# Down projection of a gated feed-forward: eleven Strassen pairs in groups of six and five in place of two plain blocks and ten pairs

## The chip, the cores and the metric

One core of one Trainium2 chip runs the whole program. The metric is device microseconds (us) of one execution on that core. Engines are named as the profile names them: PE (TensorE matmuls), PEld (its weight loads), DVE (VectorE), ACT (ScalarE), POOL (GpSimd), SP (SyncE, which here issues most of the loads).

## What is computed

A trunk of two layers over 1024 tokens of width 1024: differential attention in layer 0, latent attention in layer 1, each followed by a gated feed-forward with a causal convolution of width 3; one RMSNorm at the end. What the change touches is the last product of the feed-forward:

```python
def conv_ffn(h, w_up, conv_w, conv_b, w_down):
    u = h @ w_up
    c = lax.conv_general_dilated(
        u, conv_w[:, None, :].astype(u.dtype), window_strides=(1,),
        padding=[(CONV_WIDTH - 1, 0)], dimension_numbers=('NWC', 'WIO', 'NWC'),
        feature_group_count=u.shape[-1]) + conv_b
    g, val = jnp.split(c, 2, axis=-1)
    return (jax.nn.silu(g) * val) @ w_down      # (1024 x 2816) @ (2816 x 1024)

for i in range(DEPTH):                           # DEPTH = 2
    ...
    x = x + conv_ffn(h, ffn_w_up[i], ffn_conv_w[i], ffn_conv_b[i], ffn_w_down[i])
```

## The kernel before

**Numbers.** Everything is fp32. A factor is split into a high part (`hi`, L128, a cast on ACT) and a low part (`lo`, L131, a subtraction on DVE), and a product is three matmuls of 128x512, `mm3`, at L120, L121 and L122. So each new factor of 128x512 costs one cast on ACT and one subtraction on DVE.

**Down projection** (`down`). The hidden width 2816 is 22 blocks of 128 rows. Gated blocks arrive from the up projection through HBM: the convolution's `store` (L1097) writes block f to `g_d[f]` from ACT's queue, and `fetch` (L1265) loads halves of it, and of the weight rows, on SP's queue. Two neighbouring blocks form a pair, four quarters A11 to A22 of 128x512 of the gated values and four, B11 to B22, of the weights. A pair's product is made by seven products M1 to M7 of 128x512 factors (Strassen-Winograd) in place of eight; their factors (`DOWN`) are quarters or sums of quarters (`SUMS`; S1 to S4 of A, T1 to T4 of B), made on DVE (L1275). One M of one pair is 12 matmuls: four token tiles by three. The pairs are worked in groups: for each M, in the order `FOLLOW` (M2, M1, M5, M6, M3, M7, M4), all pairs of the group are added up in PSUM banks, and then `evict` (L1441) adds the four banks to the resident residual tiles X on DVE. M3, M6, M7 and M4 go on in the banks of an earlier M (`ONTO`), so they wait until those have been read. `todo` lists the products in this order, numbered i from 0.

**The two plain blocks.** 22 blocks are eleven pairs, but before the change only ten pairs are worked so, in groups of five and five (`GROUPS`). Blocks 0 and 1 are plain: their 96 matmuls per layer (two blocks, eight token tiles, two halves, three each) stand first, right behind the last product of the up projection. Four of their sixteen tiles lie in the first M2's banks, and the other twelve are taken by adds into X (`taken`, L1387).

**Up projection's closing.** At the point where the down projection's matmuls begin, the last hidden block f=21 is not ready yet. `pieces` (handed over as `before`) are its remaining steps: `closing` (L1203, an add on DVE that reads the temporary `U2`), the convolution's base and taps (L1084, L1088), `silu` (L1091), `gated` (L1094) and `store` (L1097). `down` calls one piece after each of its first products.

**What sets the order.** SP's order is written out: from the first fetch to the middle of the plain products its queue runs in the order of the program (`manual_schedule` over SP). ACT's order is likewise the program's in the up projection and its closing (`region`). `advance(i + DEPTH - 1)` prepares the factors of products ahead: cast, subtraction and then the sums that `MAKE` (keyed by the product's number in its group) puts there, at most two steps at a call. Tile names: u, s and h tiles are places in SBUF, S, b and u (as a matmul's output) are PSUM. In SP's rows `s<-x_d` is a load of 1 MB of the residual X (L1321), `<-g_d` and `<-in_ffn_down` are quarters of 256 KB. A DMA's landing is counted on one of eight counters, named DMAHW0 to DMAHW7 in the order of instructions, taken in turn; a new DMA on a counter waits for the last one's landing there.

Of the kernel before, what the change touches and what calls it, by code (L numbers as in the profile page):

```python
# [56 lines left out]
class Trunk:  # L57
# [946 lines left out]
    def up(self, layer, pl, g_d, follow):  # L1004
# [214 lines left out]
    GROUPS = (range(1, 6), range(6, 11))  # L1219
# [10 lines left out]
    MAKE = {4 + j: [(j, "S1"), (j, "T1")] for j in range(5)}  # L1230
    MAKE |= {o: [(x // 4, ("S3", "T3", "S2", "T2")[x % 4]) for x in xs] for o, xs in zip(range(9, 18), (range(0, 3), range(3, 6), *(range(i, i + 2) for i in range(6, 20, 2))))}
    for j in range(5):
        MAKE.setdefault(18 + j, []).append((j, "S4"))
        MAKE.setdefault(23 + j, []).append((j, "T4"))

    LAST = (0, 2, 1, 3)

    LIE = {"A12": (0, 0), "B21": (0, 1), "A11": (1, 0), "B22": (1, 1), "A22": (2, 0), "B11": (2, 1), "A21": (3, 0), "B12": (3, 1)}
    LIE2 = {"A12": "A11", "B21": "B11", "A11": "A12", "B11": "B22", "A21": "A21", "B12": "B12", "A22": "A22", "B22": "B21"}

    NEXT = {"M3": ["A12", "A11", "B11"], "M7": ["B21", "A21", "B12"], "M4": ["A22", "B22"]}

    def down(self, layer, pl, g_d, x_d, done, ahead):
# [3 lines left out]
        ring, temps = self.ring(*pl.down), self.ring(*[f"h{i}" for i in (9, 8, 3, 0, 5, 6, 7, 4, 1, 2)])  # L1247
# [10 lines left out]
        def fetch(j, name):  # L1258
            unit, half = self.LIE[name if j < 6 else self.LIE2[name]]
            k = (j - 1) % 5, unit  # L1260
            if k not in places:
                place = pl.units[unit][k[0]]
                places[k] = self.at(place, [P, D]) if isinstance(place, str) else place()
            blocks[j, name] = places[k][:, half * 512 : half * 512 + 512]
            nc.sync.dma_start(blocks[j, name], source(j, name))  # L1265

        def value(j, name):

            if name not in self.SUMS:
                return blocks[j, name]  # L1270
            if (j, name) not in made:
                x, y, op, place = self.SUMS[name]
                x, y = value(j, x), value(j, y)
                made[j, name] = temps([P, 512]) if place is None else blocks[j, place]
                nc.vector.tensor_tensor(made[j, name], x, y, op)  # L1275
            return made[j, name]

        def sums(i):
            n, o = divmod(i, len(todo) // 2)
            if n < 2:  # L1280
                for x, name in self.MAKE.get(o, ()):
                    value(self.GROUPS[n][x], name)

# [7 lines left out]
        def low(i):  # L1291
# [6 lines left out]
            if n == 0:  # L1298
                for name in self.NEXT.get(m, []):
                    fetch(j + 5, name)  # L1300
# [14 lines left out]
        X, raws, plain = [], [], []  # L1315
# [7 lines left out]
        def fetch_plain(src, *pieces):  # L1323

            w = D // len(pieces)
            for x, piece in enumerate(pieces):
                nc.sync.dma_start(piece, src[:, x * w : x * w + w])
            raws.append(pieces)

        def high_plain(i):  # L1330
            plain.append(ring([P, 2, D], F32R))
            w = D // len(raws[i])
            for x, piece in enumerate(raws[i]):
                self.hi(plain[i][:, 0, x * w : x * w + w], piece)

        def low_plain(i):
            w = D // len(raws[i])
            for x, piece in enumerate(raws[i]):
                c = slice(x * w, x * w + w)
                self.lo(plain[i][:, 1, c], piece, plain[i][:, 0, c])  # L1340


        w_down = a["ffn_down"][layer]
        order = self.tc.manual_schedule(engines={mybir.EngineType.SP})
        order.__enter__()
        unit = lambda i: self.at(pl.raw[i], [P, D])
# [5 lines left out]
        fetch_plain(g_d[1], self.at(pl.w[4], [P, D]))  # L1352
        fetch_plain(w_down[P : 2 * P, :], self.at("h12", [P, 512]), self.at("h13", [P, 512]))
        high_plain(1)
        yield
        def fetch_all(j, *names):
            for name in names:
                fetch(j, name)

        fetch_all(1, "A12", "B21")  # L1360
        yield
        fetch_all(2, "A12", "B21")
        fetch_all(3, "A12", "B21")
        high_plain(2)
        yield
        low_plain(0)
        low_plain(1)
        fetch_x(1)
        high_plain(3)
        yield  # L1370
        low_plain(2)
        fetch_all(4, "A12", "B21")
        fetch_x(1)
        yield
        low_plain(3)
        fetch_x(1)
        fetch_all(5, "A12", "B21")
        fetch_x(1)
        for j in range(1, 6):
            fetch_all(j, "A11", "B11")  # L1380
        fetch_all(1, "A21", "B12", "A22")
# [7 lines left out]
        two = [self.big() for _ in range(2)]  # L1389
        ahead_of = [s[:, cols] for s in two for cols in (first, rest)]  # L1390

        def plain_product(out, t, b, j, last):
            g, w = plain[j : j + 2]
            tok, cols = slice(t * P, t * P + P), slice(b * 512, b * 512 + 512)
            self.mm3(out, g[:, 0, tok], g[:, 1, tok], w[:, 0, cols], w[:, 1, cols], j == 0, last)

        older = []
        pairs = [[(0, 1), (1, 1)], [(2, 1), (3, 1)]] + [[(t, 0), (t, 1)] for t in range(4, NT)]
        for x, pair in enumerate(pairs):
            now = [(at_, self.bank("u" if x % 2 and b else "b")) for b, at_ in enumerate(pair)]  # L1400
            both = [(2 * x + q, ahead_of[2 * x + q]) for q in range(2)] if x < 2 else []
            for j in (0, 2) if x == 0 else (None,):
                for q, out in both:
                    for i in (0, 2) if j is None else (j,):
                        plain_product(out, q, 0, i, False)
                for (t, b), out in now:
                    for i in (0, 2) if j is None else (j,):
                        plain_product(out, t, b, i, i == 2)
            taken(older)
            older = now  # L1410
            if before:
                for f in before.pop(0):
                    f()
            if x:
                if x > 1:
                    low(x - 2)
                high(x - 1)
# [915 lines left out]
```

## Time and profile before

| what | before |
| --- | --- |
| median of 3 runs (lowest, highest) | 2365.13 us (2365.07, 2366.61) |
| the profiled execution: its own time, its span | 2365.86 us, 2364.0 us |
| PE busy | 2342.8 us (99% of the span), 12146 matmuls |
| DVE busy | 1898.2 us (80%) |
| ACT, POOL busy | 1252.7 us (53%), 577.6 us (24%) |
| first plain matmul of the down projection, layer 0 | 980.95 us |

Times are read from the profiled execution, on its own clock, which starts with the span. Where the text names a time such as +2.7, it counts from 980.95 us, the start of the down projection's matmuls in layer 0 (called its start below).

### The profile page before, as it was taken

Reading aid. Unit: us, or ns where it says so; the run is one execution under the profiler, and the core shown is the slowest. Engines: PE = TensorE matmul, PEld = TensorE weight load, DVE = VectorE, ACT = ScalarE, POOL = GpSimd, SP = SyncE. Lnnn points to the kernel's source line nnn. Section 1 sums busy time; section 2 is a strip of 40 time slices with the busy share of each in tenths; the row PEclk is TensorE's granted clock in tenths of the full one; section 3 lists DMA queues with packets and bytes.
Section 4 is the critical chain, followed back from the end, with each engine's and each line's share of the span. In section 5 each row is a group of like instructions: output and inputs, shape, how many; then the busy total and the mean of one; then the engine's idle time right before and its main releaser. Section 6 shows DMA issues by size and latency. Waiting matters only on the chain.

```text
span 2364.0 us, 32924 instructions
## 1 busy us (share of the span) xinstructions
PE 2342.8 (99%) x12146; PEld 1977.4 (84%) x12146; DVE 1898.2 (80%) x3148; ACT 1252.7 (53%) x2308; POOL 577.6 (24%) x464
## 2 busy tenths in 40 slices
PE   9999999999999999999999999999999999999998
PEld 7888888788888888888899889988888888888887
DVE  6777878859888888899844888886588888888997
ACT  5666666745444444444444777775454444444444
POOL 4545444323000000000132666664420000000001
PEclk9999999999999999999999999999999999999999
DMA  4111111342222222643222211124322222228502
GB/s 148 41 37 37 49 37 54 112 134 87 93 84 81 80 81 89 231 149 118 93 82 63 72 31 41 41 88 120 105 79 90 88 81 80 81 86 288 170 10 81
DMA packets 95665, 213.42 MB, mean 90 GB/s; under 512 B 8712, under 2 KB 33936, under 8 KB 95504
## 3 DMA queue, kind: packets, MB, share of 16 engines
q1 hardware_dynamic: 86304, 183.51, 23.6%
q10 hardware_dynamic: 9200, 27.80, 3.2%
q8 instruction: 96, 1.57, 0.3%
q14 instruction: 65, 0.53, 0.1%
HBM read 158.85 MB, written 52.43 MB: 89 GB/s over the span
## 4 chain that ended last, share of the span: by engine, by line
PE 94%; DVE 3%; DMA 1%; ACT 1%; issue 1%; POOL 0%; POOLq 0%; ACTq 0%; DVEq 0%; SPq 0%
PE S L122 14%; PE S L120 14%; PE S L121 13%; PE b L120 9%; PE b L121 9%; PE b L122 9%; PE u L120 5%; PE u L122 5%; PE u L121 5%; PE S L1878 3%; PE b L264 2%; PE u L2034 1%; PE b L1924 1%; PE u L2033 1%; DVE s L131 1%
## 5 line engine op out<-in xcount | busy, mean ns | idle before, releaser
L168 POOL TENSOR_TENSOR st<-st,mhalf 128x1 f32<-128x1 f32 x56 | 33.0, 590 | 1288.6 <-DVE st L165 1273.5
L120 PE MATMUL S<-s,u 128*128 128x512 f32 (+1 forms) x800 | 302.1, 378 | 0.2 <-ACT u L1110 0.2
L122 PE MATMUL S<-s,u 128*128 128x512 f32 (+1 forms) x800 | 301.5, 377 | 0.1
L121 PE MATMUL S<-s,u 128*128 128x512 f32 (+1 forms) x800 | 301.4, 377 | 0.0
L128 ACT CAST u<-h 128x512 fp32r<-128x512 f32 (+1 forms) x194 | 115.8, 619 | 266.7 <-DVE h L1031 262.8
L120 PE MATMUL b<-s,u 128*128 128x512 f32 x588 | 231.0, 393 | 1.1 <-DVE u L131 0.4
L122 PE MATMUL b<-s,u 128*128 128x512 f32 x588 | 229.3, 390 | 0.0
L121 PE MATMUL b<-s,u 128*128 128x512 f32 x588 | 229.3, 390 | 0.0
L1088 DVE SCALAR_TENSOR_TENSOR u<-u,conv,u 128x1023 f32<-128x1023 f32 (+1 forms) x176 | 225.0, 1279 | 0.8 <-ACT u L1084 0.7
L128 ACT CAST s<-u 128x512 fp32r<-128x512 f32 (+3 forms) x253 | 157.0, 658 | 123.1 <-issue 25.2
L150 POOL TENSOR_TENSOR u<-u,st 128x512 f32<-128x512 f32 (+7 forms) x160 | 173.3, 1092 | 160.8 <-DVE st L2019 107.9
L128 ACT CAST u<-b 128x512 fp32r<-128x512 f32 (+1 forms) x256 | 134.8, 547 | 92.3 <-PE b L1924 57.7
L131 DVE TENSOR_TENSOR u<-b,u 128x512 fp32r<-128x512 f32 (+1 forms) x256 | 158.6, 631 | 23.8 <-ACT u L128 22.6
L120 PEld LDWEIGHTS S<-s,u 128*128 128x128 f32 x800 | 150.6, 188 | 27.9 <-ACT u L1110 0.5
L122 PEld LDWEIGHTS S<-s,u 128*128 128x128 f32 x800 | 150.6, 188 | 27.7 <-DVE u L131 0.3
L121 PEld LDWEIGHTS S<-s,u 128*128 128x128 f32 x800 | 150.7, 188 | 27.3
L131 DVE TENSOR_TENSOR s<-u,s 128x512 fp32r<-128x512 f32 (+2 forms) x229 | 157.9, 729 | 14.6 <-ACT s L128 14.5
L120 PE MATMUL u<-s,s 128*128 128x512 f32 (+1 forms) x404 | 163.7, 405 | 1.1 <-DVE s L131 0.9
L122 PE MATMUL u<-s,s 128*128 128x512 f32 (+1 forms) x404 | 156.9, 388 | 0.0
L121 PE MATMUL u<-s,s 128*128 128x512 f32 (+1 forms) x404 | 156.3, 387 | 0.0
L1091 ACT ACTIVATE u<-u 128x1024 f32<-128x1024 f32 x44 | 46.7, 1062 | 200.3 <-DVE u L1088 200.3
L131 DVE TENSOR_TENSOR u<-h,u 128x512 fp32r<-128x512 f32 x171 | 118.1, 691 | 32.4 <-ACT u L128 31.5
(291 smaller groups left out, 6336.5 us busy)
## 6 DMA issues: line engine op xcount, KB each, us to landing
u<-in_ffn_up SPq DMA_DIRECT2D x88, 512.0 KB, 4.1
g_d<-u ACTq DMA_DIRECT2D x44, 512.0 KB, 2.6
u<-g_d SPq DMA_DIRECT2D x64, 256.0 KB, 4.9
u<-in_ffn_down SPq DMA_DIRECT2D x64, 256.0 KB, 5.2
s<-in_da_wqkv SPq DMA_DIRECT2D x23, 512.0 KB, 3.3
x_d<-u SPq DMA_DIRECT2D x16, 512.0 KB, 2.6
s<-x_d SPq DMA_DIRECT2D x8, 1024.0 KB, 10.8
u<-in_x SPq DMA_DIRECT2D x8, 512.0 KB, 6.2
```

Source lines behind the costliest of these rows:

```text
L120: mm(out, lh, rl, start=first, stop=False, skip_group_check=onto)
L121: mm(out, lh, rh, start=False, stop=False, skip_group_check=onto)
L122: mm(out, ll, rh, start=False, stop=last, skip_group_check=onto)
L128: self.nc.scalar.copy(out, src)
L131: (eng or self.nc.vector).tensor_sub(out, src, hi.bitcast(F32))
L150: self.nc.gpsimd.tensor_mul(x, x, s.to_broadcast(list(x.shape)))
L168: nc.gpsimd.tensor_tensor(r, s, self.mhalf, ALU.pow)
L264: self.nc.tensor.transpose(ps[:, j * P : (j + 1) * P], probs[t][:, k : k + P], self.ident)
L1088: nc.vector.scalar_tensor_tensor(t[half][:, back:], u[half][:, : S - back], w, t[half][:, back:], ALU.mult, ALU.add)
L1091: nc.scalar.activation(t[0], t[0], AF.Silu)
L1878: nc.tensor.matmul(sc[c][:, b : b + m], q[rows, qp, qs], kt[rows, kp, :m], start=x == 0, stop=x == 2)
L1924: k.nc.tensor.transpose(ps[:, j * P : (j + 1) * P], self.e[t][0][:, c : c + P], k.ident)
```

## The change

The plain blocks go; blocks 0 and 1 become pair 0, and the eleven pairs are worked in groups of six and five. The first M2 takes the plain products' place behind the up projection: with the first product none is issued, with the second pairs 0 and 1 are issued together (`now`). Per layer that is 84 matmuls for blocks 0 and 1 in place of 96. The adds of `taken` go (12 per layer), as do the five subtractions of the plain factors; seven products of pair 0 bring 14 subtractions and eight sums. All sums are made in place, in a quarter that is no longer wanted, so that the h tiles that held S1 and T1 are free for quarters of pairs 0, 1 and 5. `MAKE` becomes `plan`: in a group of six, S3, S1 and T1 of pair j are made at product 10 + j, S2 and T2 at 16 + j, S4 and T3 at 22 + j, T4 at 28 + j. `advance` makes one step at a call for the first six products and two after. The ring of prepared factors keeps eight places, the places of the quarters (`pl.units`) are new. Cut to its core (the lines of `evict` and of the sums are L1383 and L1282 in the changed kernel, fetches L1272 and L1329; lines up to L1211 are as before):

```diff
-    GROUPS = (range(1, 6), range(6, 11))
+    GROUPS = (range(6), range(6, 11))
...
-        "S1": ("A21", "A22", ALU.add, None), "T1": ("B12", "B11", ALU.subtract, None),
-        "S3": ("A11", "A21", ALU.subtract, "A21"), "S2": ("A22", "S3", ALU.subtract, "A11"), "S4": ("A12", "S2", ALU.subtract, "A12"),
-        "T3": ("B22", "B12", ALU.subtract, "B12"), "T2": ("T3", "B11", ALU.add, "B11"), "T4": ("B21", "T2", ALU.subtract, "B21"),
+        "S3": ("A11", "A21", ALU.subtract, "A11"), "S1": ("A21", "A22", ALU.add, "A21"), "T1": ("B12", "B11", ALU.subtract, "B11"),
+        "S2": ("A22", "S3", ALU.subtract, "A21"), "T2": ("B22", "T1", ALU.subtract, "B11"), "S4": ("A12", "S2", ALU.subtract, "A12"),
+        "T3": ("B22", "B12", ALU.subtract, "B12"), "T4": ("B21", "T2", ALU.subtract, "B21"),
...
+    def plan(self, size):
+
+        plan = {}
+        for j in range(size):
+            for o, names in ((2 * size - 2, ("S3", "S1", "T1")), (3 * size - 2, ("S2", "T2")), (4 * size - 2, ("S4", "T3")), (5 * size - 2, ("T4",))):
+                plan.setdefault(o + j, []).extend((j, name) for name in names)
+        return plan
...
-        ring, temps = self.ring(*pl.down), self.ring(*[f"h{i}" for i in (9, 8, 3, 0, 5, 6, 7, 4, 1, 2)])
+        ring = self.ring(*pl.down)
...
-                made[j, name] = temps([P, 512]) if place is None else blocks[j, place]
+                made[j, name] = blocks[j, place]
...
-        fetch_plain(g_d[0], unit(0))
-        fetch_plain(w_down[:P, :], unit(1))
+        fetch_all(range(4), "A12", "B21")
         yield
-        high_plain(0)
+        high(0)
         yield
...
+        fetch_all([4], "A12", "B21")
+        high(1)
         yield
...
+        fetch_all([5], "A12", "B21")
         yield
...
+        fetch_all([0, 1], "A11", "B11")
+        high(2)
         yield
...
+        low(0)
+        low(1)
+        fetch_all([2], "A11", "B11")
         fetch_x(1)
-        high_plain(3)
+        high(3)
         yield
...
+        low(2)
+        fetch_all([3, 4], "A11", "B11")
         fetch_x(1)
         yield
...
+        low(3)
+        high(4)
+        fetch_all([5], "A11", "B11")
+        fetch_all(range(4), "A21", "B12", "A22", "B22")
+        fetch_x(2)
         before, region = yield
-
-        def taken(pairs):
-            for (t, b), y in pairs:
-                x = X[t // 2][:, t % 2, b * 512 : b * 512 + 512]
-                nc.vector.tensor_add(x, x, y)
...
                 for j in group:
+                    now = [j]
+                    if i < 2:
+                        now = group[:2] if i else []
                     for q in range(4):
-                        products(banks[m][q], n, m, j, q, group)
+                        for x in now:
+                            products(banks[m][q], n, m, x, q, group)
+                    if before:
+                        for f in before.pop(0):
+                            f()
+                        if not before:
+                            fetch_all([4, 5], "A21", "B12", "A22", "B22")
+                            order.__exit__(None, None, None)
...
-                    advance(i + DEPTH - 1)
+                    advance(i + DEPTH - 1, 1 if i < len(self.GROUPS[0]) else 2)
...
-            down=slots(0, 1, 4, 5, 13, 12, 10, 11), X=slots(2, 3, 6, 7),
+            down=slots(0, 1, 10, 11, 12, 4, 5, 13), X=slots(2, 3, 6, 7),
...
+        pl.units = [[("h12", "h13"), ("h3", "h0"), "u14", "u15", "u9", "u0"], [("h1", "h2"), *units(1, 12, 4, 5, 13)],
+                    ["u11", s8[1], s9[1], "u3", "u7", "u6"], ["u10", s8[0], s9[0], "u8", "u2", ("h4", "h5")]]
```

How the instructions stand shows at three places, all in layer 0 around the up projection's closing. A row's last part names the semaphores that it waits for.

SP, in the change, from the last fetches for M2 on (h_1597 and h_1598 are pair 0's A11 and B11, in the temporaries h1 and h2; h2 has held the `U2` that `closing` reads; L1329 is a load of X; u_1604 and u_1605 are A11 and B11 of pairs 3 and 4, s_1612 the A21, A22, B12 and B22 of pair 1):

```order
L1272 DMA h_1597_9156<-g_d_142 128x512 [waits DMAHW5_49,DVE_49]
L200 DMA h_1742_10868<-in_mla_g 128x384 [waits DMAHW6_49,DVE_49]
L1272 DMA h_1598_9157<-in_ffn_down 128x512 [waits DMAHW0_49,DVE_49]
L1272 DMA u_1599_9160<-g_d_142 128x512 [waits DMAHW1_49,PE_49]
L1272 DMA u_1599_9160<-in_ffn_down 128x512 [waits DMAHW2_49]
...
L1329 DMA s_1602_9188<-x_d_139 128x2x1024 [waits DMAHW5_49,PE_49]
...
L1329 DMA s_1606_9215<-x_d_139 128x2x1024 [waits DMAHW2_49]
...
L1272 DMA s_1612_9247<-in_ffn_down 128x512 [waits DMAHW2_49]
L1272 DMA s_1612_9247<-g_d_142 128x512 [waits DMAHW3_49]
L1272 DMA s_1612_9247<-in_ffn_down 128x512 [waits DMAHW4_49]
```

Behind the fetch into h_1598 stand, in the change, 17 fetches of 256 KB and two loads of X up to and with the row of s_1612 that takes the counter DMAHW3. The same queue before, at the place where the plain blocks' fetches end:

```order
L1265 DMA u_1596_9150<-in_ffn_down 128x512 [waits DMAHW2_49]
L1321 DMA s_1598_9172<-x_d_139 128x2x1024 [waits DMAHW3_49,PE_49]
L1265 DMA u_1600_9192<-g_d_142 128x512 [waits DMAHW4_49]
L1265 DMA u_1600_9192<-in_ffn_down 128x512 [waits DMAHW5_49]
L1321 DMA s_1601_9195<-x_d_139 128x2x1024 [waits DMAHW6_49]
L1321 DMA s_1603_9215<-x_d_139 128x2x1024 [waits DMAHW7_49,PE_49]
```

Before, none of these rows waits for DVE; in the change the third row of the piece waits for it, and the loads of X stand behind that row.

ACT, in the change, around the store of the last hidden block (s_1625 is product 9, s_1631 product 10, s_1636 product 11):

```order
L128 CAST s_1625_9357<-u_1604_9209 128x512 [waits DMAHW6_49,PE_49]
L128 CAST s_1625_9357<-u_1604_9209 128x512 [waits DMAHW7_49]
L1097 DMA g_d_142<-u_1580_9067 128x1024 [waits DMAHW3_49,DVE_49]
L128 CAST s_1631_9394<-u_1605_9212 128x512 [waits DMAHW0_49,PE_49]
L128 CAST s_1631_9394<-u_1605_9212 128x512 [waits DMAHW1_49]
L128 CAST s_1636_9415<-u_1609_9238 128x512 [waits PE_49]
```

The store waits for a landing on the counter DMAHW3, as it does before; what has moved is which transfer that is (the row of s_1612 above), and that the casts of products 10 and on stand behind it.

## Rows read from the trace of the kernel before

**Rows 1.** The page: span, busy time of each engine, PE's granted clock by slice, chain by engine

```profile
span 2364.0 us, 32924 instructions
...
PE 2342.8 (99%) x12146; PEld 1977.4 (84%) x12146; DVE 1898.2 (80%) x3148; ACT 1252.7 (53%) x2308; POOL 577.6 (24%) x464
...
PEclk9999999999999999999999999999999999999999
...
PE 94%; DVE 3%; DMA 1%; ACT 1%; issue 1%; POOL 0%; POOLq 0%; ACTq 0%; DVEq 0%; SPq 0%
```

**Rows 2.** PE's waits: total us, times, longest us

```profile
PE b L500 <- DMA u<-in_attn_norm_g: 3.2, 1, 3.2
PE S L120 <- ACT u L2013: 1.8, 3, 1.3
```

**Rows 3.** Windows: us, busy us by engine, granted clock, DMA share, GB/s

```profile
0.00:8.20 8.20, 4.77 (x16) 3.93 (x16) 1.68 (x5) 5.52 (x10) 1.88 (x10) 1.00 0.77 291
960.00:980.00 20.00, 20.00 (x90) 16.57 (x89) 17.78 (x22) 11.13 (x16) 0.00 (x0) 1.00 0.63 210
980.00:1000.00 20.00, 20.00 (x90) 16.54 (x90) 15.52 (x22) 6.96 (x10) 0.00 (x0) 1.00 1.04 379
1000.00:1040.00 40.00, 40.00 (x178) 33.15 (x177) 40.00 (x66) 17.39 (x32) 0.00 (x0) 1.00 0.41 143
1040.00:1080.00 40.00, 40.00 (x179) 33.12 (x177) 39.45 (x67) 18.77 (x34) 0.00 (x0) 1.00 0.71 237
2160.00:2200.00 40.00, 40.00 (x178) 33.16 (x177) 40.00 (x66) 18.64 (x33) 0.00 (x0) 1.00 0.49 177
2360.00:2364.00 4.00, 0.00 (x0) 0.00 (x0) 0.35 (x1) 0.32 (x1) 0.00 (x0) 0.50 0.37 138
```

**Rows 4.** Timeline of PE, down projection: start us, us, engine, line, tile

```profile
980.95 0.39 PE L120 MATMUL S<-s,s 128*128 128x512 f32 x1
...
983.67 0.39 PE L120 MATMUL S<-s,s 128*128 128x512 f32 x1
```

**Rows 5.** Timeline of SP, start of the down projection, layer 0

```profile
980.60 0.37 SPq L1321 DMA_DIRECT2D s<-x_d  x1
...
982.61 0.33 SPq L1265 DMA_DIRECT2D u<-in_ffn_down  x1
986.64 0.32 SPq L1265 DMA_DIRECT2D u<-g_d  x1
989.39 0.33 SPq L1265 DMA_DIRECT2D u<-in_ffn_down  x1
...
995.29 0.32 SPq L1265 DMA_DIRECT2D s<-g_d  x1
995.98 0.33 SPq L1265 DMA_DIRECT2D s<-in_ffn_down  x1
...
998.01 0.34 SPq L1265 DMA_DIRECT2D u<-g_d  x1
998.69 0.35 SPq L1265 DMA_DIRECT2D u<-in_ffn_down  x1
```

**Rows 6.** Timeline of DVE, the up projection's closing, layer 0

```profile
982.96 0.68 DVE L1203 TENSOR_TENSOR u<-S,h 128x512 f32<-128x512 f32 x1
```

**Rows 7.** L1265's fetches, time from a DMA's issue to its landing

```profile
DMA to landing us min/median/max: 2.5/5.2/13.9
```

**Rows 8.** Timeline of ACT, the last store and the casts around it

```profile
998.57 2.17 ACT L128 CAST s<-u 128x512 fp32r<-128x512 f32 x4
1003.47 0.35 ACTq L1097 DMA_DIRECT2D g_d<-u  x1
1003.92 2.19 ACT L128 CAST s<-u 128x512 fp32r<-128x512 f32 x4 [3.19 <-DVE u L1094]
```

**Rows 9.** Timeline of DVE, sums and subtractions with no wait between them

```profile
1099.91 0.69 DVE L1275 TENSOR_TENSOR h<-u,u 128x512 f32<-128x512 f32 x1
...
1102.32 0.69 DVE L1275 TENSOR_TENSOR h<-u,u 128x512 f32<-128x512 f32 x1
```

More of the change, by code (lines that the diff above doesn't have):

```diff
@@ L1241 @@
-    NEXT = {"M3": ["A12", "A11", "B11"], "M7": ["B21", "A21", "B12"], "M4": ["A22", "B22"]}
+    LIE = {"A12": (0, 0), "B21": (0, 1), "A11": (1, 0), "B11": (1, 1), "A21": (2, 0), "B12": (2, 1), "A22": (3, 0), "B22": (3, 1)}
+    LIE2 = {"A12": "A21", "B21": "A12", "A11": "B22", "B11": "B11", "A21": "A11", "B12": "B12", "A22": "A22", "B22": "B21"}
+    NEXT = {"M3": ["A12", "B21", "A11"], "M7": ["B11", "A21", "B12"], "M4": ["A22", "B22"]}
     def down(self, layer, pl, g_d, x_d, done, ahead):
         nc, a = self.nc, self.a
-        ring, temps = self.ring(*pl.down), self.ring(*[f"h{i}" for i in (9, 8, 3, 0, 5, 6, 7, 4, 1, 2)])
+        ring = self.ring(*pl.down)
@@ L1258, in fetch @@
         def fetch(j, name):
-            unit, half = self.LIE[name if j < 6 else self.LIE2[name]]
-            k = (j - 1) % 5, unit
+            size = len(self.GROUPS[0])
+            unit, half = self.LIE[name if j < size else self.LIE2[name]]
+            k = j % size, unit
             if k not in places:
                 place = pl.units[unit][k[0]]
-                places[k] = self.at(place, [P, D]) if isinstance(place, str) else place()
-            blocks[j, name] = places[k][:, half * 512 : half * 512 + 512]
+                if isinstance(place, tuple):
+                    places[k] = [self.at(x, [P, 512]) for x in place]
+                else:
+                    tile = self.at(place, [P, D]) if isinstance(place, str) else place()
+                    places[k] = [tile[:, :512], tile[:, 512:]]
+            blocks[j, name] = places[k][half]
             nc.sync.dma_start(blocks[j, name], source(j, name))
@@ L1273, in value @@
                 x, y = value(j, x), value(j, y)
-                made[j, name] = temps([P, 512]) if place is None else blocks[j, place]
+                made[j, name] = blocks[j, place]
                 nc.vector.tensor_tensor(made[j, name], x, y, op)
             return made[j, name]
+        plans = [self.plan(len(group)) for group in self.GROUPS]
         def sums(i):
[L1279 to L1282, printed above, removed]
+            n = int(i >= 7 * len(self.GROUPS[0]))
+            for x, name in plans[n].get(i - n * 7 * len(self.GROUPS[0]), ()):
+                value(self.GROUPS[n][x], name)
         def high(i):
@@ L1297, in low @@
                 self.lo(w[:, part + 1, :], value(j, name), w[:, part, :])
-            if n == 0:
+            if n == 0 and j + len(self.GROUPS[0]) in self.GROUPS[1]:
                 for name in self.NEXT.get(m, []):
-                    fetch(j + 5, name)
+                    fetch(j + len(self.GROUPS[0]), name)
             elif j == self.GROUPS[1][-1]:
@@ L1313, in advance @@
                 most -= 1
-        X, raws, plain = [], [], []
+        X = []
         def fetch_x(n):
@@ L1321, in fetch_x @@
                 nc.sync.dma_start(X[t], x_d[t * 256 : (t + 1) * 256, :].rearrange("(t p) d -> p t d", p=P))
[L1323 to L1343, printed above, removed]
+        def fetch_all(js, *names):
+            for j in js:
+                for name in names:
+                    fetch(j, name)
         order = self.tc.manual_schedule(engines={mybir.EngineType.SP})
         order.__enter__()
-        unit = lambda i: self.at(pl.raw[i], [P, D])
@@ L1373, in down @@
+        fetch_all([3, 4], "A11", "B11")
         fetch_x(1)
         yield
[L1375 to L1381, printed above, removed]
-        before, region = yield
-        def taken(pairs):
-            for (t, b), y in pairs:
-                x = X[t // 2][:, t % 2, b * 512 : b * 512 + 512]
-                nc.vector.tensor_add(x, x, y)
-        two = [self.big() for _ in range(2)]
@@ L1390, in down @@
[L1390 to L1417, printed above, removed]
-            if x == 4:
-                for j in range(2, 6):
-                    fetch_all(j, "A21", "B12", "A22")
-                for j in range(1, 6):
-                    fetch(j, "B22")
-                order.__exit__(None, None, None)
@@ L1435, in products @@
             onto = m in self.ONTO
-            self.mm3(y, w[:, 0, tok], w[:, 1, tok], w[:, 2, :], w[:, 3, :], j == group[0] and not onto and (n, m) != (0, "M2"), j == group[-1], onto)
+            self.mm3(y, w[:, 0, tok], w[:, 1, tok], w[:, 2, :], w[:, 3, :], j == group[0] and not onto, j == group[-1], onto)
         def evict(n, m, *qs):
@@ L1452, in down @@
                     banks[m] = banks[self.ONTO[m]]
-                elif n == 0 and m == "M2":
-                    banks[m] = ahead_of
                 elif m != "M1":
```

28 lines of the change are left out of this document (3 added, 25 removed).

## Prediction

> **What bounds the kernel now.** I read the page first. The span is 2364.0 us, PE is busy in 2342.8 us of it, and 94% of the chain that ended last is PE's [rows 1]; the longest wait that PE has anywhere is 3.2 us, at the very beginning [rows 2]. So the kernel is bound by matmuls, and the first thing to count is how many of them go. The second thing is who stands next in line. The page's average for DVE, 80%, does not tell that; the windows do. In the down projection PE is busy in the whole of each window, and DVE is busy for 40.00 of 40.00 us from 1000 to 1040, 39.45 in the next 40, and 40.00 again from 2160 to 2200 in layer 1 [rows 3]. The reader should see two engines that are both full in the same stretch: PE because it is the bound, DVE because it prepares factors ahead as fast as it can. Work that is put on DVE there, or a late start of DVE's work, soon stops PE. The third view is SP's timeline around the up projection's closing, where the DMAs run at 379 GB/s with a busy share of 1.04 [rows 3, 5]: there the loads are the bound of whatever waits for them.
>
> **What goes.** Twelve matmuls of a product take 983.67 - 980.95 = 2.72 us, 0.227 us each [rows 4]. The change takes out 12 per layer, 24 in all: 24 x 0.227 = **5.4 us less**. PE is without a gap there, so the gain is whole if nothing else stops PE. Measured times of this kernel can tell some 0.2%, 4.7 us, from no change, so even the whole gain is only just visible.
>
> **What DVE has to do.** Per layer DVE loses 12 adds and 5 subtractions and gains 14 subtractions and 8 sums. That is 5 more instructions, and the adds that went were in the first 25 us, while what comes stands later. One instruction of 128x512 follows the next after (1102.32 - 1099.91) / 4 = 0.602 us [rows 9]. From the subtractions of product 10 up to the eviction of M7 in the group of six, DVE has 64 subtractions (products 10 to 41, two each), 48 sums (six pairs, eight each) and 16 adds of evictions (M1, M5, M6, M3): 128 instructions, 128 x 0.602 = 77.1 us. PE may begin M4 on the banks of M7 only when these 128 and the first add of M7's eviction (0.7 us) are done. M4 is the 37th product, due 36 x 2.72 = 97.9 us after the down projection's start. So PE is on time if DVE begins on product 10 by 97.9 - 0.7 - 77.1 = +20.1.
>
> **When can DVE begin on product 10?** Follow what it waits for. (1) SP's fetch of pair 0's B11 goes into h2, which `closing` still reads; that add ends at 982.96 + 0.68 = 983.64, +2.7 [rows 6]. SP runs in order, so 17 fetches of 256 KB and two loads of 1 MB of X queue behind that fetch; before, the last of the four loads of X was issued at 980.60 already [rows 5]. (2) A fetch lands at the earliest 2.5 us after its issue [rows 7]: +5.2. (3) Then the queue drains. Fetches of 256 KB are issued 0.68 to 0.69 us apart where they wait for each other's landing, and the issues around the loads of X show gaps of 2.75 and 4.03 us [rows 5]; I take 0.68 for a fetch and 3.2 for a load of X, which lies between the two gaps and nearer to the 2.8 us that 1 MB takes at 379 GB/s. 17 x 0.68 + 2 x 3.2 = 18.0 us, +23.2. The bounds: all 6.55 MB at 379 GB/s take 17.3 us; with 0.69 and 4.03 they take 19.8. (4) The last of them is the one whose counter ACT's store of the last hidden block waits for, and the casts of product 10 stand behind the store. From the store's issue to the next cast it takes 1003.92 - 1003.47 = 0.45 us, and a cast takes 2.17 / 4 = 0.54 [rows 8]: **+24.2**. DVE's own work would let it begin earlier: M2's banks are full at 6 x 2.72 = +16.3, four adds and two subtractions later it is +19.9. So it stands idle for some 4 us that it needs.
>
> [...]
>
> **What comes on top.** Pair 4's A22, for its sum S1 behind product 14, stands behind nine more fetches, the last two loads of X, the store of 512 KB (1.4 us at 379 GB/s) and two fetches of pair 4 itself, with itself 12 in all. It lands at 23.2 + 12 x 0.68 + 2 x 3.2 + 1.4 = +39.2; DVE, with four steps of five instructions, two subtractions and S3 behind it, is there at 24.2 + 23 x 0.602 = +38.0, and waits 1.1 us. Six sums stand right behind the one whose input they overwrite, and cannot overlap with it: 6 x (0.69 - 0.60) = 0.5 us. Sum: 24.2 + 77.1 + 1.1 + 0.5 + 0.7 = +103.6 against +97.9: PE begins M4 **5.7 us late**, in part already through shorter waits in M5, M6 and M3. In the second group DVE has 138 instructions, 83.1 us, in 35 x 2.72 = 95.2 us of PE, so it catches up, and nothing is lost there. Both layers have the same places and rates.
>
> **Edits that I cost at nothing.** The 128x512 casts and subtractions for the first M2 stand in the up projection's last 20 us, where DVE works 17.8 and ACT 11.1 us [rows 3]; if that cover is gone, DVE's `closing` comes later and all of the chain above with it, us for us. The first M2 needs only pairs 0 and 1 at the start and writes the same two PSUM tiles in the same rhythm as the plain products did, so I see no gap where the projections meet. Small loads of the next layer that SP's queue moves past are wanted only behind the whole down projection.
>
> **The sum.** 2 x 5.7 - 5.4 = +6.0 us. The profiled execution took 2365.86 us and would take 2371.9; it stands 0.7 above the median of 2365.13, from which it is **2371.1 us**. By the bounds: loads in 17.3 us and none of the waits on top make product 10 begin at +23.5 and PE 3.4 us late, 2366.5 us; loads in 19.8 us make it 7.5 us late, 2374.7 us. Forecast: slower, own range 2366.5 to 2374.7, chance 0.57.
>
> **Rival 1, the other side: DVE is not held and PE keeps its gain.** Its place is ACT's store: if the loads land such that the casts of product 10 are through by +19.9, DVE has no hole but M2's eviction, and PE is late by 0 to 1.4 us a layer (the waits on top): 2359.7 to 2362.5 us. It decides at +21.2 if the waits on top remain, where the loss of 2.7 us a layer equals what the matmuls give; each us earlier gains one per layer. For it: DVE was full before too and PE had no wait there. Against: DVE had X early and was not behind then; now it is two links further down a full queue. Chance 0.25, a third of it below 2360.4 us.
>
> **Rival 2: the loads land later.** Landing took up to 13.9 us where fetches and loads of X were mixed [rows 7]; a gap of 4.03 us for each of the four loads of X, 3.3 us per layer above my sum with those behind, gives 2377.7 us; half of it 2374.4. Chance 0.12.
>
> **Rival 3: PE's waits cost its clock.** [...] Waits like those forecast (2 us at most at a time) did not lower it [rows 2]. [...] Chance 0.03. [...]
>
> The remaining 0.03 I leave to what I have not thought of, without an effect. That the change does not do what it says is excluded by the order of the instructions.
>
> **How the numbers follow.** Of the forecast's 0.57 about 0.42 lie above 2369.9 (slower by over 0.2%) and 0.15 within; rival 1 gives 0.08 faster and 0.17 no difference; rivals 2 and 3 are slower. Slower 0.57, within 0.35, faster 0.08. The range goes from 2361.5, inside rival 1, to 2377.0, near rival 2's end.
>
> **What would show it.** Right: PE has 12,122 matmuls; PE waits of some us, for DVE, stand in M5, M6, M3 and at M4 of the group of six, 5 to 6 us in all per layer and none in the group of five; SP waits for the DVE add of L1203; ACT's store is issued some 23 us after the down projection's start, with ACT idle ahead of it, and DVE has a hole before product 10. Wrong: a store before +20, or a PE without waits (rival 1); waits of PE for something else than DVE or in the up projection; a granted clock below 1.00 behind a wait (rival 3).

## The result, and the profile after

The change made the kernel slower: 2373.71 us (median of 7 runs, 2373.11 to 2374.66) against 2365.77 us before (median of 7, 2365.07 to 2366.61), a ratio of 1.0034 with a 95% interval of 1.0022 to 1.0046. That is +7.9 us where +6.0 was forecast; 2373.7 lies in the range and in the forecast's own range of 2366.5 to 2374.7, near its upper end. The execution whose profile follows has a span of 2371.8 us, 7.8 us more than the one before.

The page of the changed kernel, the lines that answer to those of [rows 1]:

```profile
span 2371.8 us, 32941 instructions
...
PE 2342.5 (99%) x12122; PEld 1970.3 (83%) x12122; DVE 1902.0 (80%) x3158; ACT 1261.1 (53%) x2326; POOL 578.6 (24%) x464
...
PEclk9999999999999999999999999999999999999999
...
PE 86%; DVE 9%; DMA 3%; ACT 1%; issue 1%; POOL 0%; SPq 0%; POOLq 0%; DVEq 0%; ACTq 0%
```

PE's busy time fell by only 0.3 us although 24 matmuls went, and in the chain PE has 86% where it had 94%, DVE 9% where it had 3%. The chain now leads through DVE's work. PE's waits (total us, times, longest), to be read beside [rows 2]:

```profile
PE b L120 <- DVE s L131: 3.2, 3, 1.5
PE b L500 <- DMA u<-in_attn_norm_g: 3.1, 1, 3.1
PE b L120 <- DVE s L1383: 2.9, 2, 1.4
```

The waits for L131 (subtractions) and L1383 (evictions) are new; the wait of 3.1 us at the start is the old one. The list shows 6 us of new waits, fewer than there are: where PE waits only for some tenths of a us, the row counts it as a longer matmul (from 1000 to 1040, below, PE counts as busy for 37.89 us with 159 matmuls, which at 0.227 us make 36.1). The starts tell it better. I summed all gaps between starts of matmuls beyond 0.227 us from the down projection's start to M4: 6.5 us in layer 0 and 6.4 in layer 1, and 12.9 - 5.4 = +7.5 us is nearly the whole of the +7.8. In the kernel before, the same sum is 0. The windows of layer 0 (us, busy us by engine with instructions, granted clock, DMA share, GB/s), beside [rows 3]:

```profile
980.00:1000.00 20.00, 20.00 (x89) 16.38 (x88) 17.02 (x24) 10.07 (x15) 0.00 (x0) 1.00 0.83 304
1000.00:1040.00 40.00, 37.89 (x159) 28.78 (x158) 34.83 (x58) 13.89 (x25) 0.00 (x0) 1.00 0.55 210
1040.00:1080.00 40.00, 39.77 (x176) 32.62 (x175) 40.00 (x68) 22.00 (x40) 0.00 (x0) 1.00 0.62 202
1080.00:1120.00 40.00, 38.55 (x171) 31.62 (x170) 34.13 (x57) 14.85 (x26) 0.00 (x0) 1.00 0.19 62
```

From 1000 to 1040 PE issued 159 matmuls where the window before had 178, and DVE, full before, was idle for 5 us of 40. The granted clock is 1.00 throughout. What DVE waited for stands in its timeline, around the eviction of M2 (start us, us, engine, line):

```profile
982.89 0.68 DVE L1203 TENSOR_TENSOR u<-S,h 128x512 f32<-128x512 f32 x1
...
994.87 1.22 DVE L1094 TENSOR_TENSOR u<-u,u 128x1024 f32<-128x1024 f32 x1
996.21 1.28 DVE L1383 TENSOR_TENSOR s<-s,S 128x512 f32<-128x512 f32 x2
999.53 1.28 DVE L1383 TENSOR_TENSOR s<-s,S 128x512 f32<-128x512 f32 x2 [2.04 <-DMA s<-x_d]
1000.74 1.28 DVE L131 TENSOR_TENSOR s<-u,s 128x512 fp32r<-128x512 f32 x2
1006.98 1.29 DVE L131 TENSOR_TENSOR s<-u,s 128x512 fp32r<-128x512 f32 x2 [4.96 <-ACT s L128]
```

The down projection starts at 980.89 in this execution. DVE waits 2.0 us for the second load of X and then 5.0 us for ACT's casts of product 10, which it begins at 1006.98, +26.1. ACT's timeline there:

```profile
994.94 1.24 ACT L128 CAST s<-u 128x512 fp32r<-128x512 f32 x2 [0.79 <-DMA u<-g_d]
1005.63 0.33 ACTq L1097 DMA_DIRECT2D g_d<-u  x1
1006.33 2.18 ACT L128 CAST s<-u 128x512 fp32r<-128x512 f32 x4 [10.15 <-PE u L122]
```

ACT stands still from 996.2 to 1005.63, +24.7, where it issues the last store; what the store writes was ready at 996.1, when DVE's `gated` (L1094) ended. The row of the casts names a matmul of PE as the releaser of 10 us of idle time; the matmuls whose place in the ring these casts take, product 2's, had ended at about 989.1 (an estimate: 3 x 2.72 us behind the start, PE without a gap), and the casts stood behind the store. And SP, ahead of all of it:

```profile
969.86 0.38 SPq L1272 DMA_DIRECT2D h<-g_d  x1
...
983.61 0.33 SPq L1272 DMA_DIRECT2D h<-in_ffn_down  x1
...
985.93 0.38 SPq L1329 DMA_DIRECT2D s<-x_d  x1
...
989.40 0.37 SPq L1329 DMA_DIRECT2D s<-x_d  x1
...
1000.14 0.32 SPq L1272 DMA_DIRECT2D s<-g_d  x1
...
1011.65 0.32 SPq L1272 DMA_DIRECT2D u<-g_d  x1
```

```profile
SPq L1272 <- DVE u L1203: 9.0, 1, 9.0
```

The fetch of pair 0's B11 into h2 goes out at 983.61, when `closing` has ended; SP had waited 9.0 us for that add. The first load of X is issued at 985.93, where before the last of four was out at 980.60 [rows 5]. The fetch whose counter the store shares is issued at 1000.14 and lands 5.4 us later, at 1005.55; the store follows at 1005.63. In this trace none of the 468 DMAs for which the landing ahead on their counter is known was issued before it. Pair 4's A22 is issued at 1011.65.

### The profile page after: what moved, and what is told of

The parts are those of the page before. It is cut to its first block, busy times and chain, and to the rows that moved or that the text cites. A ratio compares the mean times of both kernels' runs of the same rounds, so it can differ in the third digit from the quotient of the medians.

```text
span 2371.8 us, 32941 instructions
## 1 busy us (share of the span) xinstructions
PE 2342.5 (99%) x12122; PEld 1970.3 (83%) x12122; DVE 1902.0 (80%) x3158; ACT 1261.1 (53%) x2326; POOL 578.6 (24%) x464
## 4 chain that ended last, share of the span: by engine, by line
PE 86%; DVE 9%; DMA 3%; ACT 1%; issue 1%; POOL 0%; SPq 0%; POOLq 0%; DVEq 0%; ACTq 0%
PE S L122 12%; PE S L120 12%; PE S L121 12%; PE b L120 8%; PE b L121 8%; PE b L122 8%; PE u L120 5%; PE u L122 4%; PE u L121 4%; DVE s L131 3%; PE S L1828 3%; PE b L264 2%; DVE u L1282 2%; PE u L1984 2%; PE u L1983 1%; PE b L1874 1%
## 5 line engine op out<-in xcount | busy, mean ns | idle before, releaser
L128 ACT CAST s<-u 128x512 fp32r<-128x512 f32 (+3 forms) x273 | 166.5, 646 | 161.1 <-DVE u L1282 69.2
L131 DVE TENSOR_TENSOR s<-u,s 128x512 fp32r<-128x512 f32 (+2 forms) x249 | 167.4, 709 | 27.0 <-ACT s L128 26.8
L131 DVE TENSOR_TENSOR u<-b,u 128x512 fp32r<-128x512 f32 (+1 forms) x256 | 158.6, 631 | 23.8 <-ACT u L128 22.7
L120 PE MATMUL u<-s,s 128*128 128x512 f32 (+1 forms) x392 | 158.9, 405 | 1.1 <-DVE s L131 0.9
L122 PE MATMUL u<-s,s 128*128 128x512 f32 (+1 forms) x392 | 152.0, 388 | 0.0
L121 PE MATMUL u<-s,s 128*128 128x512 f32 (+1 forms) x392 | 151.4, 386 | 0.0
L131 DVE TENSOR_TENSOR u<-h,u 128x512 fp32r<-128x512 f32 x171 | 118.1, 691 | 32.4 <-ACT u L128 31.5
```

The lines of the kernel that those rows point to most:

```text
L120: mm(out, lh, rl, start=first, stop=False, skip_group_check=onto)
L121: mm(out, lh, rh, start=False, stop=False, skip_group_check=onto)
L122: mm(out, ll, rh, start=False, stop=last, skip_group_check=onto)
L128: self.nc.scalar.copy(out, src)
L131: (eng or self.nc.vector).tensor_sub(out, src, hi.bitcast(F32))
```

## The experiments

Eleven kernels ran, each compared with the kernel before on the same chip. "Late" is the sum of PE's gaps in layer 0, from the down projection's start to M4's, read as above.

| run | B11's place | last stores from | other edit | median us | ratio to before (95%) | PE late, us |
| --- | --- | --- | --- | --- | --- | --- |
| the change | h2 | ACT | | 2373.71 | 1.0034 (1.0022 to 1.0046) | 6.5 |
| e1 | h6 | ACT | | 2362.55 | 0.9986 (0.9977 to 0.9995) | 1.9 |
| e2 | h2 | ACT, later | | 2374.18 | 1.0036 (1.0024 to 1.0048) | 7.8 |
| e3 | h2 | ACT | T3, T4 left out | 2369.37 | 1.0013 (1.0004 to 1.0022) | 4.3 |
| e4 | h2, fetched later | ACT | | 2369.03 | 1.0012 (1.0003 to 1.0022) | 4.0 |
| e5 | h6 | ACT | 12 more sums | 2378.62 | 1.0054 (1.0040 to 1.0067) | 9.1 |
| e6 | h2 | POOL | | 2371.85 | 1.0024 (1.0014 to 1.0035) | 6.5 |
| e7 | h6 | POOL | | 2361.03 | 0.9979 (0.9970 to 0.9988) | 0.1 |
| e8 | h6 | ACT | T3, T4 on POOL | 2376.07 | 1.0043 (1.0030 to 1.0055) | 7.2 |
| e9 | h2, fetched later | POOL | | 2361.65 | 0.9982 (0.9972 to 0.9991) | 0.3 |
| e10 | h2 | POOL | X's last loads last | 2364.50 | 0.9993 (0.9984 to 1.0003) | 2.8 |
| e11 | h2 | ACT | X's last loads last | 2373.83 | 1.0034 (1.0021 to 1.0047) | 7.3 |

**The theory** is the prediction's: `closing` holds SP's queue through h2, and the late queue makes DVE late. Its rivals, called A and B below: the group of six is too much for DVE anyway, and the loads cannot run faster anyway.

**e1: the hold taken away.**

```diff
-  pl.units = [[...], [("h1", "h2"), ...
+  pl.units = [[...], [("h1", "h6"), ...        # both layers
```

> Edit: pair 0's B11 lies in h6, which nothing reads any more at that time, in place of h2, so that SP's fetch of it has no add of DVE to wait for. Theory (that wait holds SP's queue for 9 us, and everything else follows from it): the store of the last hidden block is issued when its own input is ready, about 15 to 16 us after the down projection's start in place of 24.7; DVE runs without a hole from M2's eviction on; PE is late by 0 to 1.4 us a layer; time 2365.8 - 5.4 + (0 to 2.8) = 2360.4 to 2363.2 us. Rival A (the work itself: 128 instructions and sums in place are too much for DVE in the group of six, wherever the loads land): PE stays some 6 us late per layer, 2372 to 2374. Rival B (the loads cannot run faster): SP issues earlier, but landings move by 1 or 2 us only, 2369 to 2372.

Measured: 2362.55 us, 11.2 us less than the change and faster than before. SP's timeline of this run:

```profile
968.60 0.38 SPq L1272 DMA_DIRECT2D h<-g_d  x1
969.03 0.42 SPq L1272 DMA_DIRECT2D h<-in_ffn_down  x1
...
974.38 0.38 SPq L1329 DMA_DIRECT2D s<-x_d  x1
```

Both of pair 0's fetches go out together, and the first load of X at 974.38 in place of 985.93. So one name in a table of places was the cause of nearly all the loss; rivals A and B are out. The last store goes out at 997.59, 18.0 us after this run's start at 979.62, where 15 to 16 was expected, and PE still waits once, at M4:

```profile
PE b L120 <- DVE s L1383: 1.4, 1, 1.4
```

The reason stands in ACT's and DVE's timelines:

```profile
983.07 0.33 ACTq L1097 DMA_DIRECT2D g_d<-u  x1
983.45 1.25 ACT L1084 ACTIVATE u<-u,conv 128x1024 f32<-128x1024 f32 x1 [6.03 <-DMA u<-g_d]
```

```profile
984.72 1.28 DVE L1088 SCALAR_TENSOR_TENSOR u<-u,conv,u 128x1023 f32<-128x1023 f32 x1 [2.41 <-ACT u L1084]
...
997.24 2.47 DVE L1383 TENSOR_TENSOR s<-s,S 128x512 f32<-128x512 f32 x4
999.64 2.49 DVE L131 TENSOR_TENSOR s<-u,s 128x512 fp32r<-128x512 f32 x4
1002.04 0.68 DVE L1282 TENSOR_TENSOR h<-h,u 128x512 f32<-128x512 f32 x1
```

In this run ACT's store of the last block but one waited for a landing, ACT was idle for 6.0 us, the convolution's base (L1084) came late, and DVE idled for 2.4 us ahead of the tap. The lead that DVE lost there is PE's 1.9 us at M4, where at most 1.4 was expected; e7 below takes the cause away. By these two numbers DVE had a lead of some 0.5 us (an estimate).

**e2 and e6: the store's link alone.** The prediction's sum had named two links behind the hold: the store with the casts behind it, which bring DVE to pair 4's sum at +38.0, and the landing of pair 4's A22 at +39.2. The expectations of e2 and e6 call the store the sum's link. By the sum itself the landing ended last, so a store eased alone should have gained nothing, which is their second case.

```diff
 # e2
-  pieces = [..., [], [before.gated, before.store]]
+  pieces = [..., [], [before.gated], [], [], [before.store]]
-                        if not before:
+                        if i == 5:
 # e6
-                nc.scalar.dma_start(g_d[f], u[0])
+                (nc.gpsimd if f >= NF - 2 else nc.scalar).dma_start(g_d[f], u[0])
```

> Edit: the last hidden block's store is issued three products later, behind the casts of products 10 to 14; SP's wait for the add of closing stays. If ACT's store is the link that counts, as the sum of the prediction has it (the casts of product 10 behind the store are the only thing that is late), DVE begins product 10 some 5 us earlier and PE is late by 1 to 2 us a layer: 2363 to 2365. If the loads behind SP's hold are late by themselves, DVE only stops a little later, at the sums of pair 4 or 5, whose quarters land about 40 us after the start whatever ACT does, and little is gained: 2371 to 2374.

Measured: 2374.18, no gain, as for the second case of the expectation. But the run is not clean. DVE's waits in layer 0 and two rows of SP:

```profile
DVE u L1282 <- DMA u<-g_d: 4.7, 2, 2.8
DVE s L1383 <- DMA s<-x_d: 2.0, 1, 2.0
DVE u L1282 <- DMA h<-g_d: 1.4, 1, 1.4
```

```profile
1008.75 0.34 SPq L1272 DMA_DIRECT2D u<-in_ffn_down  x1
1017.96 0.32 SPq L1272 DMA_DIRECT2D u<-g_d  x1
```

SP stood for 9 us ahead of the fetch of pair 4's A22. The store, now issued at 1011.30, had taken the counter that this fetch uses, and SP waited 7.8 us for the store to land. So a shared counter held up SP's queue for ACT's store here, and ACT's queue for a fetch of SP in the change, where the store was ready at 996.1 and went out at 1005.63, 0.08 us behind the landing. Hence e6, where the stores use POOL's queue:

> Edit: the last two hidden blocks are stored from POOL's queue in place of ACT's; the hold of SP stays. This is the store's link taken out alone, which the run with the later store did not do cleanly: there SP's fetch of pair 4's A22 shared a counter with the store and waited for it. If ACT's store is the link (as the prediction's sum has it), DVE begins product 10 at +20 to +21 and PE is late by 1 to 2 us a layer: 2363 to 2365. If the landings behind SP's hold are late by themselves, DVE begins product 10 earlier but waits at pair 4's sums, some 39 us after the start: 2371 to 2373.5.

Measured: 2371.85 (single runs from 2368.56 to 2374.57), the second case again. The traced execution is the slowest of the seven, 2.7 us above their median, so its waits, and the 6.5 us in the table, are longer than those of a typical one. DVE's waits:

```profile
DVE u L1282 <- DMA u<-g_d: 3.5, 3, 2.5
DVE s L1383 <- DMA s<-x_d: 3.0, 1, 3.0
DVE u L1282 <- DMA h<-g_d: 0.4, 1, 0.4
```

The 5.0 us for ACT are gone, and in their place DVE waits 3.0 us for X and 3.9 us for quarters of pairs 0, 4 and 5. A link was taken out, and the next one took over. In the change the two were 1.6 us apart: pair 4's A22 landed at 1019.88, +39.0, and DVE came to the sum that needs it at 1021.46, +40.6.

**e11 and e10: the landings' link alone, and both.**

```diff
-        fetch_x(2)
         before, region = yield
...
                             fetch_all([4, 5], "A21", "B12", "A22", "B22")
+                            fetch_x(2)
```

e11 has this edit, e10 that of e6 as well.

> Edit: only the order of the last two loads of X, as in the run before; the stores are on ACT's queue as in the change. Theory (the store alone keeps PE late): DVE begins product 10 at about +26 as in the change, its sums wait for no landing, PE late by 5 to 6.5 us a layer, 2371 to 2373.5. If only the landings of pairs 4 and 5 counted, and the store not: 2361.5 to 2364.

> Edit: SP's hold as in the change; the last two stores from POOL's queue; and the last two loads of X (2 MB) stand behind the fetches of pairs 4 and 5 in place of ahead of them. Theory (two links hang on the same hold, the store ahead of the casts of product 10 and the landings of pairs 4 and 5, and either alone keeps PE late): with both eased PE is late by 0.5 to 1.5 us a layer, 2361.5 to 2364. If the hold costs its time wherever DVE stands: 2370 to 2373.

Measured: e11 2373.83, no gain (0.3 us above its range); e10 2364.50, 9.3 us less. With e6 and the change that is a square: taking out the store's link gives 1.9 us between the medians, with e6's single runs 6 us apart; taking out the landings' link gives nothing, taking out both 9.2 us. DVE's waits, e11 first, then e10:

```profile
DVE s L131 <- ACT s L128: 9.4, 5, 5.0
DVE s L1382 <- DMA s<-x_d: 2.7, 1, 2.7
```

```profile
DVE s L1382 <- DMA s<-x_d: 2.9, 1, 2.9
...
DVE u L1282 <- DMA u<-g_d: 0.2, 1, 0.2
```

In e11 the casts hold DVE for 5.0 us as in the change. In e10 neither does, and what is left is a third link of the same hold, 2.9 us for the second load of X, which M2's eviction needs; e10 came out 0.5 us above its range; I had not counted that link.

**e4 and e9: less of the queue behind the hold.**

```diff
-        fetch_all([0, 1], "A11", "B11")
+        fetch_all([1], "A11", "B11")
...
         fetch_all([2], "A11", "B11")
         fetch_x(1)
+        fetch_all([0], "A11", "B11")
```

> Edit: pair 0's A11 and B11 are fetched behind those of pairs 1 and 2 and the first load of X, still into h1 and h2; so the add of closing still holds SP, but four fetches and 1 MB of X are already out when it does. Theory (what counts is how much of the queue stands behind the hold): the queue ends some 4 x 0.68 + 3.2 = 5.9 us earlier, so the landings that DVE waits for do too; PE is late by 1 to 2.5 us a layer in place of 6.5: 2362 to 2366. If the hold's length as such counted, whatever stands behind it: no change, 2373 to 2374.

Measured: 2369.03, a gain of 4.7 us in place of the 8 to 12 expected: a miss. DVE waited for no landing in this run, but the store went out at 1003.07 only, and the casts behind it left one hole:

```profile
992.94 2.17 ACT L128 CAST s<-u 128x512 fp32r<-128x512 f32 x4
1003.07 0.33 ACTq L1097 DMA_DIRECT2D g_d<-u  x1
```

```profile
998.68 1.29 DVE L131 TENSOR_TENSOR s<-u,s 128x512 fp32r<-128x512 f32 x2
1004.14 1.29 DVE L131 TENSOR_TENSOR s<-u,s 128x512 fp32r<-128x512 f32 x2 [4.18 <-ACT s L128]
```

e9 is e4 with the stores on POOL's queue.

> Edit: the run with the hold later in the queue, and the last two stores from POOL's queue as well. In that run DVE waited for no landing; its one hole, 4.2 us before product 10, was ACT's store. Theory (with less behind the hold the landings are in time, and the store alone kept PE 4 us late): DVE begins product 10 some 4 us earlier, PE late by 0 to 0.8 us a layer, 2360.5 to 2362.5. If something else keeps it late: 2367 to 2369.

Measured: 2361.65, PE late by 0.3 us. In e4 and e9 `closing` still held SP for 7.0 us (9.0 in the change). So such a hold costs next to nothing when little that is urgent stands behind it and the stores go by POOL's queue; with the stores on ACT's queue, e4, PE was still 4.0 us late.

**e3, e5 and e8: is DVE's count of instructions the bound?**

```diff
 # e3: T3 and T4 of the group of six are not made
+                if name not in ("T3", "T4") or j >= len(self.GROUPS[0]):
+                    nc.vector.tensor_tensor(made[j, name], x, y, op)
 # e5, on top of e1: S3 and S1 made a second time
+                if name in ("S3", "S1") and j < len(self.GROUPS[0]):
+                    nc.vector.tensor_tensor(self.at("h7", [P, 512]), x, y, op)
 # e8, on top of e1: T3 and T4 on POOL
+                eng = nc.gpsimd if name in ("T3", "T4") and j < len(self.GROUPS[0]) else nc.vector
```

> Edit: in the group of six the sums T3 and T4 are not made (M7 and M4 are computed with B12 and B21 in their place); 12 instructions of DVE fewer per layer, all of them behind M6's factors. Everything else as in the change. Theory (PE waits at M3, M7 and M4 because DVE has too many instructions ahead of them): the waits up to M6's first product stay, those at M3 and M4 go, together some 2.2 us a layer: 2373.7 - 4.4 = 2369 to 2370. If DVE's count of instructions is not the bound (landings or the order of banks are): no change, 2373 to 2374.

Measured: 2369.37, as expected; PE's gaps up to M6 stay, those at M3 and M4 are gone.

> Edit: as the run with B11 in h6, and S3 and S1 of each pair of the group of six are made a second time into a free place: 12 more instructions of DVE per layer. Theory (with the hold gone DVE has next to no slack left in that group; it is just on time): 12 x 0.60 = 7.2 us per layer less a slack of 0 to 2 us, so 10 to 14 us more than that run, 2371 to 2375. If DVE has slack there: 2360 to 2365.

Measured: 2378.62, 16.1 us above e1 where 10 to 14 were expected. In layer 0 PE is 9.1 us late where e1 had 1.9: 7.2 us, 12 x 0.60, us for us. In layer 1 it is 9.0 us late where e1 had 1.0, by the same sum of gaps: 8.0 us. Together that is 15.2 of the 16.1 us. So on top of e1, where PE already waited for DVE, each instruction costs its full time; the 0.8 us more in layer 1 and the last 0.9 us stay open.

> Edit: B11 in h6, and the sums T3 and T4 of the group of six are made on POOL, which has nothing to do there, in place of DVE (12 instructions of DVE fewer per layer, output unchanged). Theory (PE's last wait, at M4, is DVE's count of instructions): it goes, 2359 to 2361. If two engines that work on SBUF at the same time slow each other down by more than the 7.2 us that DVE saves: 2362.5 or more, with DVE's steps longer than 0.60 us in the windows where POOL works.

Measured: 2376.07, 13.5 us more than e1: the second case. DVE's timeline, and POOL's row beside it:

```profile
1008.98 0.69 DVE L131 TENSOR_TENSOR s<-u,s 128x512 fp32r<-128x512 f32 x1
1009.58 1.78 DVE L131 TENSOR_TENSOR s<-h,s 128x512 fp32r<-128x512 f32 x1
```

```profile
1009.20 1.61 POOL L1283 TENSOR_TENSOR s<-s 128x512 f32<-128x512 f32 x1 [2.62 <-DMA u<-g_d]
```

POOL's sum runs from 1009.20 to 1010.81. DVE's subtraction that falls into it, with both inputs in SBUF, takes 1.78 us in place of 0.69: it ends 0.55 us after POOL's. Nine of the layer's 12 sums on POOL lengthen one DVE instruction by some 1.09 us each. Seven come ahead of 1043.70: from the sum at 1002.82 to there DVE takes 40.88 us, where e1 takes 33.25 for the same instructions (1002.04 to 1035.29), 7 x 1.09 us more. The other two are the rows of 1051.51 (1.79 us) and 1053.22 (1.77). Of the remaining three sums, two run beside evictions, which have one input in PSUM and are not lengthened (the four adds from 1048.52 on take 2.49 us, 2.48 in e1), and the third takes long itself:

```profile
1037.85 16.60 POOL L1283 TENSOR_TENSOR u<-u,u 128x512 f32<-128x512 f32 x4 [3.51 <-DVE u L1283]
```

The row merges four sums. The first of them alone takes 11.6 to 12.7 us (an estimate: the 16.60 less three sums of the 1.30 to 1.67 us that each of the eight before took), so it ends between 1049.4 and 1050.6. DVE runs subtractions and sums back to back at their usual 0.69 us until 1048.52, and from there to 1051.01 an eviction. Why these ten instructions, nine of DVE and one of POOL, took longer no run shows, only that they did while both engines worked.

What it costs is a matter of place as well as of price. POOL makes the six sums T3 from 1005 to 1028; DVE in e1 makes them from 1038 on. So seven of the nine delays, 7.6 us, come ahead of M6, and the time that DVE saves, 12 x 0.60 = 7.2 us, comes behind it. PE's gaps show it: all but 0.6 of its 7.2 us in layer 0 have come when M6 begins, at 1036.6, and none is left at M4. Against e1 the gaps of both layers give 10.0 us (7.2 + 5.7 - 1.9 - 1.0) of the 13.5; the rest I did not trace.

**e7: the version that beats both.** The edits of e1 and e6 together.

> Edit: both together, B11 in h6 and the last two stores from POOL's queue. In the run with B11 in h6 alone, PE was still 1.9 us late in layer 0, at M4, because ACT's store of the last block but one waited 6 us for a landing and the convolution's base behind it made DVE idle for 2.4 us. Theory: that idle time goes, DVE begins product 10 at +19.9, and PE has next to no wait left in the down projection: 2362.5 - 2 x (1.3 to 1.9) = 2358.7 to 2360.5, counted as 2359 to 2361. If the 128 instructions are too many for DVE anyway: no change, 2362 to 2363.

Measured: 2361.03 us, ratio 0.9979 (0.9970 to 0.9988) to the kernel before, and 12.7 us less than the change. Its windows in layer 0:

```profile
1000.00:1040.00 40.00, 40.00 (x178) 33.14 (x177) 39.79 (x66) 15.10 (x27) 0.00 (x0) 1.00 0.32 124
1040.00:1080.00 40.00, 40.00 (x178) 33.12 (x177) 40.00 (x68) 20.86 (x38) 0.00 (x0) 1.00 0.75 250
1080.00:1120.00 40.00, 40.00 (x178) 33.15 (x177) 33.83 (x56) 16.14 (x29) 0.00 (x0) 1.00 0.02 7
```

PE is busy for 40.00 of 40.00 us again in each window, with 178 matmuls in each as before, and has no wait in the down projection. 2366.03 - 2361.03 = 5.0 us is what the 24 matmuls are worth (2.8 to 7.1 by the ratio's interval), against 5.4 by the rows.

## Why the prediction came out right

- **What goes.** 24 x 0.227 = 5.4 us. Shown by e7, where nothing stops PE: 5.0 us.
- **The hold at h2.** Shown by e1: SP waited 9.0 us in the change, the fetch went out at +2.7 as said, and without the wait the kernel is 11.2 us faster. e9 shows the same with little behind the hold.
- **The queue behind it.** Forecast: store at +23.2. Measured: +24.7, within the forecast's bounds, so the term was mis-sized by 1.5 us. The trace says where. The second fetch behind the hold landed at 989.39, +8.5, where 5.2 + 2 x 0.68 = +6.6 had been put (the 2.5 us from issue to landing is the shortest of all fetches [rows 7]; the first two behind the hold took 3.4 and 4.9 us). From there to the store's counter it took 16.2 us, where 16.6 had been put. The loads of X, the term with the widest bounds, were cheaper than the 3.2 us forecast: the two landed 2.6 us after the landing ahead of them. Why the first landings came late no run shows. The rate stayed as forecast: the window from 986 to 1005 shows 376 GB/s at a DMA share of 1.02.
- **The start of product 10.** Forecast +24.2, measured +26.1: those 1.5 us, 0.7 us from the store to the cast where a row had shown 0.45, and 0.65 us for the cast where 0.54 had been put.
- **DVE from there to M4.** 77.1 + 0.5 + 0.7 us behind +26.1 make +104.4; M4 began at 1085.58, +104.7. The sums that overwrite the input of the one ahead start 0.71 to 0.72 us behind it (1008.19 to 1008.91), where 0.69 had been put. The trace has the 64 subtractions, 48 sums and 16 adds that were counted, from 1006.98 to M7's eviction at 1084.71. So the pace of 0.602 us and the count of 128 hold, and e3 and e5 show that it is the count that decides.
- **The wait for pair 4's A22.** Forecast 1.1 us, measured none. The landing came as forecast, +39.0 for +39.2, but DVE came to its sum at +40.6 in place of +38.0. The sum had taken the later of the two links, which is right; which of them is the later it had the wrong way round. e6 and e11 show that both count: with one of the two eased, the other alone keeps PE late by nearly as much as before.
- **Luck in the size.** Product 10 was begun 1.9 us later than forecast, and the forecast wait of 1.1 us did not come. Two errors partly cancelled, so M4 came only 1.1 us later than forecast in layer 0.
- **Rival 1** fell, as the store went out at +24.7. It is what e7 made come true. **Rival 2** (later landings) came true in part in its size, 1.5 us a layer of the 3.3 that it put, but not in its cause: the loads of X were no slower than forecast. **Rival 3:** no run shows a clock that a wait lowered. The granted clock stayed at 1.00 in each window with waits, whose longest in the down projection was 1.5 us; nothing was lost to the clock.
- The waits stood where they were forecast, in M5, M6, M3 and M4 of the group of six, and also in M1's last products; none in the group of five. In the sum 2 x 6.45 - 5.4 = +7.5 us, where 2 x 5.7 - 5.4 = +6.0 had been put.

## What to carry to other kernels

Before a tile is given a new place, ask who read that place last and when, and then what stands behind the load on its queue: here one fetch of 256 KB that waits 9 us for an add cost 11 us, and in another idle place (h6) it waits for nothing. When an experiment takes a link out and nothing moves, look for a second link of nearly the same length on the same cause before dropping the theory; it takes a square of runs (neither, one, the other, both) to see it. And count the instructions of the helper engine up to the point where the bound engine needs them, not its average load. Where work is moved off that engine, look at when the saving comes and when the cost: in e8 the cost came first.

## What the runs showed that I had not expected

- A landing counter that two queues shared tied them together: a store on ACT, ready at 996.1, waited 9 us for a load of SP that had nothing to do with it (until 1005.63 in the change), and a load of SP 7.8 us for a store of ACT (between 1008.75 and 1017.96 in e2).
- A sum of 128x512 moved to an idle POOL lengthened a DVE instruction with two inputs in SBUF by 1.09 us, more than the sum itself costs on DVE (0.60 us); this held for nine of 12 in layer 0 of e8. One of the others took 11.6 to 12.7 us itself (an estimate), 10.7 of them while DVE ran subtractions and sums without a gap.
- The same kind of gap may be listed as a wait or hidden in a longer matmul: of 6.5 us late in layer 0 the list of waits shows 3.1.
